# Two blocks on one core: what the order of TensorE's work does after a product on part of the array

## The chip, the cores and the metric

One core of a Trainium2 chip runs the whole program. The metric is the device time of one execution in microseconds; of the kernel before there are three runs.

## The reference, cut to what matters

256 tokens of width 1024 pass through two blocks, all in fp32. Only the parts that meet on TensorE are shown.

```
block 1:  h = rmsnorm(x);  proj = h @ w_in            # q k v z, dq dk dv
          gated delta rule, chunks of 64, 4 heads:    # "delta"
             A = I + strict(k_beta k^T * decay);  solve A [u|w] = rhs
             scan over 4 chunks: v_new = u - w S;  o = q S + a v_new;  S = S g + k^T v_new
          differential attention, 4 heads             # "diff heads"
          x += [o_la, o_d] @ w_out
          x += (silu(h @ w_gate) * (h @ w_up)) @ w_down
block 2:  mixer: gated linear attention in chunks ("gla"), block attention ("moba"), gates
          memory attention over 256 memory rows
          mixture of experts: 32 experts, 2 per token, each 1024 -> 512 -> 1024
```

## The kernel before, in words

**Dense products.** Every weight of the dense layers is fp32 and is split on chip into two fp32r parts, high and low (`Stream.split`: ScalarE rounds the high part, VectorE subtracts it for the low one). A product of activations and weights is then three matmuls: high x high, high x low, low x high. `job_ws`, `job_as`, `job_out`, `job_ffn` and `job_half` issue them in pieces of three, and give the turn back after each piece with `yield 0`. In the trace such a piece is three rows whose operands are `wh` or `wl` (weights) and `xTh`, `xTl`, `memTh` and the like; a piece has 256 or 512 columns per matmul. These jobs stand in one list, `self.jobs`, in the order of the weights' loads.

**Chains.** Everything between the dense layers (delta, diff heads, gla, moba, norms, softmax) is written as generators, called chains, which give the turn back where they have to wait. Many of their products use only part of the 128x128 array: `delta` works on chunks of 64 rows, so it multiplies 64x64 blocks on the rows 0 to 63 and 64 to 127, and the states of its scan are 64x128 or 128x64. Here such a product is called a part product, any other a dense one. In fp32 one product is two MATMUL rows, so eight products are a group of x16.

**Delta's inverse.** The triangular system is inverted by six levels of doubling (`for l in range(6)` in `delta`, L1208). In each level, for both row tiles t = 0 and 1, a first set of eight part products (`mks` by M, rows `im,mk`) goes to a bank, VectorE scales it to `pt` (rows `ipt`), and then a second set (rows `im,ipt` and `ipt,im`) and a VectorE subtraction give the next M (rows `im`). After the levels come `wT` and `u` (rows `im,kb` and `av,im`), and the scan over four chunks (rows `u,kd`/`vn,kd`, `u,KE`/`vn,KE`, `S,wT`, `S,qs`). `gla` has part products of the same sort (rows `gqs,gki`, `vg,gkdn`, `gS,gqe`).

**Who sets the order.** The program's order is fixed when it is built. `Pace` is a model of the engines: `note` (L201) charges each instruction a cost, remembers when each tensor is written (`wr`) and when each engine is free (`free`); `at` adds a latency, 205 ns from a VectorE write to TensorE. `drive` (L474) picks the next step: of the chains, in their order in the list, the first whose `ready` is not later than `now`, which is TensorE's planned free time plus 50 ns; if there is none, the first job goes on by one piece, unless a chain would be ready as early. A bare `yield` in a chain sets `ready` to the end of its step plus 200 ns (`advance`, L446), a `yield tensor` to the time at which the tensor is there for TensorE, `yield 0` to at once. So after a bare `yield` behind a product, a dense piece always goes in between, if there is one. The order on each engine's own queue is the order in which the steps are issued; `Stream.pump` puts the splits of the weights between them. The expert weights of the last part come through 22 buffers of 1 MB (`Experts`); its order is written out by hand, `drive` has no part in it.

Each row of the profile names line 249, since every instruction passes through one helper; so rows are told apart by their tiles.

Of the kernel before, what the change touches and what calls it, by code (L numbers as in the profile page):

```python
# [19 lines left out]
F32R = mybir.dt.float32r  # L20
# [14 lines left out]
class Pack:  # L35
    def __init__(self):
        self.off, self.n = {}, 0
        self.parts = []
# [93 lines left out]
TABLE = {AF.Exp: 0, AF.Ln: 1, AF.Silu: 2, AF.Sigmoid: 3}  # L132
TICK = 3413.0
NS1 = 178
NWARM = 18
NKEEP = 1
NAFT = 1
# [11 lines left out]
class Pace:  # L149
# [7 lines left out]
    def __init__(self):  # L157
        self.free = dict.fromkeys(("tensor", "vector", "scalar", "gpsimd", "sync"), 0.0)
        self.dma, self.step = 0.0, 0.0
        self.tick, self.full, self.cols = 0, False, 0.0  # L160
        self.table = None
        self.wr, self.rd = {}, {}

    def cost(self, eng, op, out, ins):
# [36 lines left out]
    def note(self, eng, op, args, kw):  # L201
        isap = lambda v: hasattr(v, "tensor") and hasattr(v, "ap")
        out = args[0]
        ins = [a for a in (*args[1:], *kw.values()) if isap(a)]
        t = self.free[eng]
        if op == "activation" and args[2] in TABLE and TABLE[args[2]] != self.table:
            t += 1283
            self.table = TABLE[args[2]]
        if op == "dma_start" and eng == "sync":
            t = max(t, self.dma)  # L210
        outs = [out] + [o for o in (kw.get("accum_out"),) if o is not None]
        if op == "tensor_tensor_reduce":
            outs.append(ins.pop())
        for a in ins:
            t = max(t, self.at(a, eng))
            if a.space == PSUM:
                t = max([t] + [e + 130 for o, e in self.rd.get(a.tensor.name, {}).items() if o != eng])
        for o in outs:
            t = max([t] + [e + (100 if n != eng else 0) for n, e in self.rd.get(o.tensor.name, {}).items()])
        if op == "dma_start":  # L220
            n = out.nbytes() / 360.0
            if eng == "sync":
                self.dma = self.free[eng] = t + n
            else:
                self.free[eng] = t + 1000
            end = t + n + 2000
        else:
            c = 165 * out.shape[-1] + 300 if kw.get("op") == ALU.pow else self.cost(eng, op, out, ins)
            if eng == "tensor":
                n, rows = out.free_size(), ins[0].shape[0]  # L230
                c = self.clock(t, c, n if rows < 128 else min(2.4 * c, 4 * n))
            end = self.free[eng] = t + c
        for o in outs:
            self.wr[o.tensor.name] = (end, eng)
        for a in ins:
            self.rd.setdefault(a.tensor.name, {})[eng] = end
        if op != "dma_start":
            self.step = max(self.step, end)
# [31 lines left out]
class Stream:  # L270
# [59 lines left out]
    def next(self, name):  # L330
        i = self.used
        assert self.pieces[i][0] == name, (self.pieces[i][0], name)
        while self.nsplit <= i:
            self.split()
        self.used += 1
        _, _, _, kk, n, _ = self.pieces[i]
        hi, lo = (w.rearrange("p (k n) -> p k n", n=n) for w in self.hl[i % HLB])
        return hi, lo, kk
# [87 lines left out]
class K:  # L426
# [47 lines left out]
    def drive(self, chains, until=None):  # L474

        until = until or chains
        chains = list(chains)
        while not all(c.done for c in until):
            chains = [c for c in chains if not c.done]
            self.jobs = [c for c in self.jobs if not c.done]  # L480
            self.S.pump()
            now = self.m.free["tensor"] + 50
            live = [c for c in chains if self.runnable(c)]
            best = next((c for c in live if c.ready <= now), None)
            if best is None:
                live += [c for c in self.jobs[:1] if self.runnable(c)]
                assert live, "no chain can go on"
                best = min(reversed(live), key=lambda c: max(c.ready, now))
            self.advance(best)
# [139 lines left out]
    def small(self, name):  # L629
        o, n = self.soff[name]  # L630
        return self.sml[0][:, o:o + n] if o < NS1 else self.sml[1][:, o - NS1:o - NS1 + n]

# [179 lines left out]
    def begin(self):  # L812
# [7 lines left out]
                    self.c2.tile([128, I["consts"].shape[1] - NC1], F32, name="cst2")]  # L820
        self.sml = [self.c2.tile([128, NS1], F32, name="sml1"),
                    self.c2.tile([128, I["small"].shape[1] - NS1], F32, name="sml2")]
        nc.sync.dma_start(self.cst[0], I["consts"][:, :NC1])
        for t, q in enumerate((nc.sync, nc.scalar)):
            q.dma_start(x[t], I["x"][0, t * 128:(t + 1) * 128, :])
        nc.sync.dma_start(self.sml[0], I["small"][:, :NS1])
        self.junk = self.c2.tile([128, 512], F32, name="junk")
        self.cut = self.c2.tile([128, 232], F32, name="cut")
        self.S = Stream(self, self.plan())
        self.S.load(2)  # L830
        nc.sync.dma_start(self.sml[1], I["small"][:, NS1:])
        nc.sync.dma_start(self.cst[1], I["consts"][:, NC1:])
        self.S.load()
        self.ident = self.const("ident")
        for _ in range(NWARM):
            self.mm(self.banks[0][:, :128], self.ones, self.ones, True, True)
# [1463 lines left out]
```

## Time and profile before

| what | value |
|---|---|
| runs of the kernel before | 1089.24, 1089.37, 1089.77 us (median 1089.37) |
| the profiled execution's own time | 1089.57 us |
| its span, first to last instruction | 1087.8 us |
| busy share: PE, PEld, DVE, ACT, POOL | 97%, 69%, 46%, 35%, 5% |
| mean granted TensorE clock | 0.997 of full speed |
| moved from and to HBM | 300 MB, mean 276 GB/s |
| chain that ended last | PE 61%, DMA 33%, DVE 2%, ACT 2% |

PE is the matmul side of TensorE, PEld its weight loads, DVE VectorE, ACT ScalarE, POOL GpSimd. A matmul's duration in the rows is longer than its distance to the next one, since matmuls are pipelined; what a matmul takes of TensorE's time is read from start to start. A row "x16" is a group of 16 matmuls; its start is the first one's.

### The profile page before, as it was taken

The numbers are of one execution on the slowest core, as the hardware profiler recorded it, in microseconds if no ns is written. First come the engines' busy times: TensorE is split into PE (matmuls) and PEld (weight loads), VectorE is DVE, ScalarE is ACT, GpSimd is POOL, SyncE is SP. The second block draws the span as 40 slices with busy tenths as digits, with TensorE's granted clock in tenths as the row PEclk, the third lists the DMA queues.
The fourth block names the chain that finished last, engine by engine and source line by source line (L and its number), as shares of the span: only waits on it lengthen the run. The fifth ranks groups of instructions, "written<-read, shape, count | busy, mean of one in ns | idle before, by whom it ended". The sixth has DMA issues, their size and how long they took to land.

```text
span 1087.8 us, 16591 instructions
## 1 busy us (share of the span) xinstructions
PE 1056.4 (97%) x6848; PEld 750.9 (69%) x6848; DVE 505.7 (46%) x919; ACT 383.5 (35%) x680; POOL 57.4 (5%) x86
## 2 busy tenths in 40 slices
PE   9999999999999999999999999999999998989995
PEld 8989788999999978889998754434443434334541
DVE  5777747665655568575577552222121212111121
ACT  6553536644434466566446430110000000000112
POOL 0145011000000010100000000000000000000000
PEclk9999999999999999999999999999999999999998
DMA  8453225576465535463559779999999999999994
GB/s 306 124 193 111 67 78 161 207 271 208 159 215 176 173 116 166 157 202 130 188 183 355 288 296 421 421 420 421 421 421 421 421 421 421 420 420 421 421 421 191
DMA packets 91100, 300.03 MB, mean 276 GB/s; under 512 B 4951, under 2 KB 33932, under 8 KB 67724
## 3 DMA queue, kind: packets, MB, share of 16 engines
q1 hardware_dynamic: 89564, 294.70, 71.1%
q0 software_dynamic: 1024, 3.17, 1.0%
q8 instruction: 56, 0.92, 0.3%
q10 hardware_dynamic: 432, 1.05, 0.3%
q14 instruction: 24, 0.20, 0.0%
HBM read 297.83 MB, written 1.07 MB: 275 GB/s over the span
## 4 chain that ended last, share of the span: by engine, by line
PE 61%; DMA 33%; DVE 2%; ACT 2%; issue 1%; POOL 0%; SPq 0%; ACTq 0%; DVEq 0%
PE bank L249 61%; DMA wm<-in_w_exp_up 20%; DMA wm<-in_w_exp_down 13%; ACT junk L249 1%; DMA x<-in_x 0%; DVE cy L249 0%; DVE junk L249 0%; DVE xTl L249 0%; ACT wh L249 0%; DVE x L249 0%; ACT xTh L249 0%; ACT sg L249 0%; ACT wm L249 0%; DVE dp L249 0%; POOL nr L249 0%
## 5 line engine op out<-in xcount | busy, mean ns | idle before, releaser
L249 DVE TENSOR_TENSOR wl<-wr,wh 128x1024 fp32r<-128x1024 f32 (+1 forms) x175 | 211.2, 1223 | 134.2 <-ACT wh L249 130.9
L249 PE MATMUL bank<-wm,xe 128*64 128x512 f32 x1024 | 231.7, 596 | 3.3 <-DMA wm<-in_w_exp_up 3.3
L249 PE MATMUL bank<-xTh,wh 128*128 128x256 f32 x768 | 223.1, 291 | 0.0
L249 ACT ACTIVATE wh<-wr 128x1024 fp32r<-128x1024 f32 (+1 forms) x175 | 180.1, 1050 | 118.4 <-PE bank L249 102.8
L249 PE MATMUL bank<-xTl,wh 128*128 128x256 f32 x768 | 217.3, 283 | 0.8 <-DVE xTl L249 0.8
L249 PE MATMUL bank<-xTh,wl 128*128 128x256 f32 x768 | 217.2, 283 | 0.2 <-DVE wl L249 0.2
L249 PEld LDWEIGHTS bank<-wm,xe 128*64 128x64 f32 x1024 | 74.7, 137 | 137.4 <-issue 123.4
L249 PEld LDWEIGHTS bank<-xTh,wh 128*128 128x128 f32 x768 | 147.0, 191 | 4.6 <-issue 2.4
L249 PEld LDWEIGHTS bank<-xTl,wh 128*128 128x128 f32 x768 | 147.1, 192 | 2.3 <-DVE xTl L249 1.2
L249 PEld LDWEIGHTS bank<-xTh,wl 128*128 128x128 f32 x768 | 147.0, 191 | 0.4 <-DVE wl L249 0.4
L249 PE MATMUL bank<-wm,hdT 128*64 128x512 f32 x512 | 118.7, 594 | 8.9 <-DMA wm<-in_w_exp_down 7.6
L249 DVE TENSOR_TENSOR sg<-bank,sg 128x512 f32<-128x512 f32 x16 | 11.1, 692 | 187.5 <-PE bank L249 187.5
L249 PEld LDWEIGHTS bank<-wm,hdT 128*64 128x64 f32 x512 | 39.7, 137 | 82.7 <-issue 64.4
L249 ACT ACTIVATE sg<-bank 128x512 f32<-128x512 f32 x20 | 11.9, 597 | 198.3 <-PE bank L249 198.2
L249 DVE SCALAR_TENSOR_TENSOR ys<-bank,ws,ys 128x512 fp32r<-128x512 f32 x32 | 24.0, 751 | 114.7 <-ACT ys L249 113.0
L249 ACT ACTIVATE ys<-bank,ws 128x512 fp32r<-128x512 f32 x32 | 22.0, 687 | 152.0 <-PE bank L249 152.0
L249 POOL TENSOR_TENSOR nr<-nr,mhalf 128x2 f32<-128x2 f32 (+1 forms) x9 | 6.0, 673 | 670.8 <-DVE nr L249 670.7
L249 PEld LDWEIGHTS bank<-ys,pwT 128*128 128x128 f32 x128 | 22.7, 188 | 18.5 <-issue 11.4
L249 PE MATMUL bank<-wl,fhh 128*128 128x512 f32 x88 | 35.2, 400 | 0.0
L249 PE MATMUL bank<-ys,pwT 128*128 128x512 f32 x128 | 34.6, 410 | 0.5 <-DVE ys L249 0.5
L249 PE MATMUL bank<-wh,fhh 128*128 128x512 f32 x88 | 34.8, 395 | 0.0
L249 PE MATMUL bank<-wh,fhl 128*128 128x512 f32 x88 | 34.5, 392 | 0.0
(384 smaller groups left out, 1445.4 us busy)
## 6 DMA issues: line engine op xcount, KB each, us to landing
wm<-in_w_exp_gate SPq DMA_DIRECT2D x64, 1024.0 KB, 19.8
wm<-in_w_exp_up SPq DMA_DIRECT2D x64, 1024.0 KB, 19.8
wm<-in_w_exp_down SPq DMA_DIRECT2D x62, 1024.0 KB, 19.8
wr<-in_w_in SPq DMA_DIRECT2D x33, 1024.0 KB, 5.2
wr<-in_w_gate_up SPq DMA_DIRECT2D x22, 1024.0 KB, 5.3
wr<-in_w_down SPq DMA_DIRECT2D x11, 1024.0 KB, 5.2
wr<-in_w_out SPq DMA_DIRECT2D x8, 1024.0 KB, 5.1
wr<-in_w_ckv SPq DMA_DIRECT2D x4, 1024.0 KB, 7.4
```

The source lines that it names most:

```text
L249: r = f(*args, **kw)
```

## The change: how chains and pieces are ordered, and what a change of kind costs in the plan

`note` now classes each TensorE instruction: dense, if it contracts over more than 64 rows and is a transpose, has more than 64 columns of weights, or is fp32r; otherwise it is a product on part of the array. An instruction whose class differs from the one before is charged 115 ns more. And `drive` moves `now` 150 ns later for the chains, if TensorE's last planned instruction was a part product.

```
+NEAR = 150
...
-        self.table = None
+        self.table, self.dense, self.was = None, True, True
...
             if eng == "tensor":
                 n, rows = out.free_size(), ins[0].shape[0]
-                c = self.clock(t, c, n if rows < 128 else min(2.4 * c, 4 * n))
+                self.dense = rows > 64 and (op == "transpose" or ins[0].shape[-1] > 64 or ins[0].dtype == F32R)
+                c = self.clock(t, c, n if rows < 128 else min(2.4 * c, 4 * n)) + (115 if self.dense != self.was else 0)
+                self.was = self.dense
             end = self.free[eng] = t + c
...
             live = [c for c in chains if self.runnable(c)]
+            if not self.m.dense:
+                now += NEAR
             best = next((c for c in live if c.ready <= now), None)
```

No instruction's shape, data or count is changed by it; only the order in which the steps are issued can be.

## Rows read from the trace of the kernel before

**Rows 1.** Windows: us; busy us (count) of each engine; clock, DMA share, GB/s.
```profile
0.00:640.00 640.00, 631.81 (x4812) 568.51 (x4813) 412.00 (x726) 335.11 (x602) 56.26 (x84) 1.00 0.56 188
640.00:645.00 5.00, 5.00 (x29) 2.02 (x29) 4.25 (x5) 2.61 (x3) 0.00 (x0) 1.00 0.00 0
645.00:1062.00 417.00, 405.78 (x1956) 175.20 (x1952) 84.21 (x180) 39.68 (x63) 0.00 (x0) 1.00 1.01 420
```

**Rows 2.** Waits of PE up to 640 us: us in total, times, longest.
```profile
PE bank L249 <- DVE x L249: 1.6, 1, 1.6
...
PE bank L249 <- POOL nr L249: 0.2, 1, 0.2
```

**Rows 3.** Windows of delta's inverse, its scan, the mixer, and one unbroken part stretch.
```profile
68.00:118.00 50.00, 50.00 (x736) 44.65 (x735) 34.55 (x59) 20.44 (x39) 22.43 (x30) 1.00 0.43 138
118.00:165.00 47.00, 46.75 (x337) 36.69 (x336) 29.84 (x90) 24.55 (x73) 5.19 (x6) 1.00 0.20 68
400.00:510.00 110.00, 109.95 (x786) 96.78 (x787) 75.38 (x152) 70.48 (x133) 9.30 (x18) 1.00 0.50 161
157.20:162.90 5.70, 5.70 (x43) 4.12 (x41) 2.71 (x11) 0.98 (x5) 0.00 (x0) 1.00 0.00 0
```

**Rows 4.** Timeline of PE, delta's inverse: start us, us, engine, line, operation, tiles.
```profile
69.33 0.50 PE L249 MATMUL bank<-wh,xTh 128*128 128x512 f32 x1
...
103.05 0.68 PE L249 MATMUL bank<-im,ipt 64*64 64x64 f32 x16
103.56 0.63 PE L249 MATMUL bank<-ipt,im 64*64 64x64 f32 x16
104.13 0.39 PE L249 MATMUL bank<-xTh,wh 128*128 128x256 f32 x1
104.35 0.28 PE L249 MATMUL bank<-xTl,wh 128*128 128x256 f32 x1
104.47 0.28 PE L249 MATMUL bank<-xTh,wl 128*128 128x256 f32 x1
104.68 0.68 PE L249 MATMUL bank<-im,ipt 64*64 64x64 f32 x16
...
106.30 0.68 PE L249 MATMUL bank<-im,mk 64*64 64x64 f32 x16
106.92 0.39 PE L249 MATMUL bank<-xTh,wh 128*128 128x256 f32 x1
...
115.89 0.39 PE L249 MATMUL bank<-xTh,wh 128*128 128x256 f32 x1
```

**Rows 5.** Timeline of DVE in the same stretch.
```profile
102.61 1.23 DVE L249 TENSOR_TENSOR wl<-wr,wh 128x1024 fp32r<-128x1024 f32 x1 [1.45 <-PE bank L249]
...
105.87 0.69 DVE L249 TENSOR_TENSOR im<-im,bank 128x512 f32<-128x512 f32 x1 [0.94 <-PE bank L249]
107.03 0.42 DVE L249 TENSOR_TENSOR ipt<-bank,lastat 128x256 f32<-128x256 f32 x1 [0.47 <-PE bank L249]
```

**Rows 6.** Timeline of PE, delta's second half.
```profile
128.74 0.50 PE L249 MATMUL bank<-wh,xTh 128*128 128x512 f32 x1
...
136.96 1.08 PE L249 MATMUL bank<-u,KE 64*64 64x128 f32 x8
137.97 1.09 PE L249 MATMUL bank<-S,wT 128*64 128x128 f32 x8
...
143.37 1.08 PE L249 MATMUL bank<-vn,KE 64*64 64x128 f32 x8
144.38 0.50 PE L249 MATMUL bank<-wh,xTh 128*128 128x512 f32 x1
...
154.01 0.39 PE L249 MATMUL bank<-memTh,wh 128*128 128x256 f32 x1
```

**Rows 7.** Timeline of PE, the mixer's gla.
```profile
436.68 0.65 PE L249 MATMUL bank<-vg,gkdn 64*64 64x128 f32 x8
437.27 0.50 PE L249 MATMUL bank<-wh,xTh 128*128 128x512 f32 x1
```

## The prediction, made before the changed kernel was built or run

> **What bounds the kernel now.** I read the windows first, cut where the expert part begins. Up to 640 us TensorE is busy for 631.8 of 640 us while the DMA engines are at 0.56; from 645 to 1062 us the DMA engines are full at 420 GB/s and stay so [rows 1]. Between them lie 5 us with no DMA at all [rows 1]: all 22 expert buffers are full and wait for the first one to be used up. So the second half is a fixed amount of loading that cannot begin before TensorE has come to the experts, and every microsecond that TensorE saves or loses before 640 us moves the end by the same amount. Next the waits of PE up to 640 us: twelve, from 1.6 down to 0.2 us, each seen once or twice [rows 2]. TensorE does not wait for others there; what it can save is time in which it is busy and does no useful work. The stages with part products are three, and PE is busy in them for 50.0 of 50, 46.75 of 47 and 109.95 of 110 us [rows 3]. So the timeline of PE, start to start, is the view that decides.
>
> **What an interposed piece costs.** In the inverse the second set of tile 0 (103.05 and 103.56) is followed by a dense piece, and that by the second set of tile 1 at 104.68 [rows 4]. The first group of 16 takes 0.51 us when another part group follows it. From 103.56 to 104.68 are 1.12 us; one group of 0.51 and three dense matmuls at the 0.12 us that stand between 104.35 and 104.47 make 0.87. So 0.25 us are lost: 0.06 on the way out of the part group, 0.10 at the first dense matmul (0.22 instead of 0.12) and 0.09 on the way back (0.21 instead of 0.12). Behind a first set the way out costs more: 106.30 to 106.92 is 0.62 against 0.51, so 0.11 [rows 4], and the loss 0.30. I take 0.28 for each piece that no longer stands between two part products. The three dense matmuls themselves are not saved: the piece is done later, in a row of others.
>
> **Where the change removes one.** A bare `yield` behind a part product made the chain ripe 200 ns after TensorE's free time, while `drive` looked 50 ns ahead; now it looks 200 ns ahead, so the chain goes on at once. Whether that brings two part products together depends on what the next step needs. I went through the chains in their order:
>
> - Inverse, between the tiles: the second set of tile 1 needs only `pt` of tile 1, finished long before. Six levels, six pieces. In level 0 the first set of tile 1 needs nothing, and in levels 1 and 2 M of tile 1 is old, as long runs of dense work stand before them: three more pieces. From level to level (three places with a single piece) tile 0's first set needs M of tile 0. That makes 12 pieces, the first at 69.33, the last at 115.89 [rows 4].
> - The last three have a wait. A set begun at 106.30 is through at 106.81 (0.51 later), and VectorE begins with it at 107.03, so 0.22 later [rows 4, 5]. Its subtraction takes 0.69 us [rows 5], the plan allows 0.205 us on to TensorE: 1.12 us, of which tile 1's two groups cover 2 x 0.51. About 0.1 us is waited. Sum for the inverse: 12 x 0.28 - 3 x 0.1 = 3.1 us.
> - From the first sets to tile 0's second set the evacuation takes 0.22 + 0.42 us [rows 5] plus 0.2, of which the other first set covers 0.51. If the plan bridges it, TensorE stands for about 0.33 us in place of losing 0.30: nothing, either way. The first set of tile 1 in levels 3 to 5 needs a fresh M and keeps its piece.
> - Delta's second half: eight pieces (three of them transposes of a diff head) go, the first at 128.74, the last at 154.01 [rows 6]: between `wT` and `u`, `u` and `wT`, `u` and the scan, `kd` and `KE`, `wT` and `qs`. After the first `KE` the scan needs a fresh S, so the piece removed in front of that `KE` comes back behind it: not counted.
> - Here the two classes of the planner are too few. `KE` (64x64) followed by `S,wT` (128x64) takes 1.01 us, and followed by a dense matmul also 1.01 us [rows 6]. Going from one part form to another costs what going to a dense one costs. Of the eight places six join unlike forms, so one change of about 0.10 stays: 6 x 0.18 + 2 x 0.28 = 1.6 us.
> - gla: three pieces between like forms, one between the two `gqs,gki` sets and two between the `vg,gkdn` sets, as at 437.27 [rows 7]: 3 x 0.28 = 0.8 us. `qkm`, `pT,vm` and `gS,gqe` stay, since the next step waits for a softmax, or there is none.
>
> The Trainium skill speaks to the fifth point ("TensorEngine Tiling (Array Packing)", section Key Properties): changing the tiling mode drains TensorE, and it means any mode, not only a step from part to whole. The trace agrees with its 1.01 against 1.01 us. If the planner's two classes were right instead, the sum would be 0.6 us larger.
>
> **What it adds.** The later `now` holds for every chain behind a part product, also for one whose next step is dense: TensorE then stands up to 150 ns longer without a part product to gain. About 30 of the 57 part stretches that the timeline has up to 640 us keep a piece behind them; I put 0.5 us on this, between 0 and 30 x 0.15 = 4.5. The instructions queued behind such a wait are only dense pieces, for which nobody waits. The 115 ns are no work; they make the plan's TensorE slower, by 57 x 0.23 = 13 us over the stage if all stayed, near the 0.25 to 0.30 measured. This moves many decisions between chains and splits; I put nothing on it, with 2 us to either side, which is what a handful of shifted pieces and waits as in [rows 2] amount to.
>
> Sum: 3.1 + 1.6 + 0.8 - 0.5 = 5.0 us, all on the path, as TensorE never waits and the DMA stream follows it. The profiled execution took 1089.57 us (1.8 outside its span), 0.2 above the median of the runs; so 1084.6 by its own time, 1084.4 against the median. A difference under 0.2% (2.2 us) I count as none.
>
> **Rivals.**
>
> 1. *The pieces come back.* A chain that goes on sooner meets its next real wait sooner, and a piece is put there; only what needs nothing is gained (the six between the tiles and three in gla, 2.5 us, less the 0.5 for waits and up to 2 of shifted order). Time 1087 to 1089.4, say 1088.3. For it: S and M are fresh after every second set. Against it: pieces already stand at those real waits, and a longer run there costs one loss, not two.
> 2. *Late operands, slower.* The plan charges 80 ns for a product that takes 0.51/8 = 64 ns [rows 4]. It believes a set of eight to last 0.13 us longer than it does, and so bridges waits longer than 200 ns; and VectorE works in order, with splits of 1.23 us [rows 5] in front of the evacuations. Each piece taken out is 0.36 us of cover gone. It decides where the wait at the some 23 places exceeds 0.28 us on average. If one in three stands behind a split: 8 x 1.23 = 9.8, less 5.5 gained, so 4.3 us slower: 1093.7. Against it: the plan counts VectorE's queue, and PE hardly waits today [rows 2].
> 3. *The clock falls.* Longer stretches of small part products with waits between them could lower the granted clock from 2.4 to 1.2 GHz. If half of the inverse's 50 us ran so, 25 us of work would take 50: 25 us less 5, 1109. Against it: 1.00 in all three stages, and in 5.7 us of part products without one dense piece [rows 3].
> 4. *More than counted.* A plan with dearer changes also sets fewer pieces at the waits I call even; five more at 0.28 and no waits: 1081.8.
>
> **How the numbers follow.** Forecast 0.55, rival 1 0.22, rival 2 0.13, rival 3 0.03, rival 4 0.07. The forecast's own range is 1082.0 to 1087.2. With rival 1 and the near end of rival 2 the range is 1081.5 to 1090.0. Faster: the forecast, rival 4 and a little of rival 1, 0.64; the same: most of rival 1, 0.21; slower: 0.15.
>
> **What would show it.** In the changed trace: MATMUL counts unchanged; in the inverse the second sets of both tiles back to back (two groups `im,ipt`/`ipt,im` with no `wh` row between); fewer part stretches, about 34 to 40 in place of 57; the first `wm` matmul about 5 us before its 640; the DMA stream at 420 GB/s for as long as before, with all of the gain ahead of it. Rival 2 shows as new PE waits for DVE `ipt` or `im`, rival 3 as a clock under 1.00 between 68 and 165. I am wrong if the stretches are fewer but the experts start no earlier.

## The result: slower, and where the time went

The changed kernel takes 1098.99 us (six runs, 1096.32 to 1101.99), the kernel before 1089.55. The ratio is 1.0088, with an interval of 1.0078 to 1.0098: 0.9% slower, where 0.5% faster was forecast. The six runs stand in two groups, 1096.3 to 1096.9 and 1101.1 to 1102.0 us, with mean granted clocks of 0.995 and 0.987, so the median lies between them, where no run is; the profile is of the first (1096.68 us, span 1094.9).

First the windows of the changed kernel, cut where its experts begin, as [rows 1] and [rows 3].

```profile
0.00:647.50 647.50, 627.11 (x4816) 568.33 (x4816) 413.66 (x726) 336.50 (x603) 51.90 (x84) 0.99 0.55 186
647.50:652.00 4.50, 4.50 (x23) 1.63 (x24) 4.39 (x5) 2.10 (x2) 0.00 (x0) 1.00 0.00 0
652.00:1069.00 417.00, 405.55 (x1956) 175.33 (x1950) 84.13 (x180) 39.68 (x63) 0.00 (x0) 1.00 1.01 420
68.00:118.00 50.00, 46.41 (x735) 43.03 (x731) 38.77 (x69) 22.03 (x44) 17.82 (x28) 1.00 0.40 128
118.00:165.00 47.00, 40.15 (x298) 33.79 (x297) 24.72 (x70) 21.13 (x62) 6.98 (x8) 0.96 0.19 58
131.00:138.00 7.00, 1.73 (x19) 1.29 (x18) 3.89 (x18) 3.72 (x14) 2.03 (x2) 0.96 0.06 23
137.40:140.80 3.40, 2.85 (x14) 2.86 (x15) 1.17 (x3) 0.00 (x0) 0.00 (x0) 0.51 0.00 0
400.20:403.70 3.50, 3.50 (x19) 3.50 (x18) 2.60 (x7) 1.87 (x6) 0.00 (x0) 0.51 0.00 0
```

The second half is as it was: 417 us of loading at 420 GB/s behind some 5 us without DMA. The experts begin 6.9 us later (647.50 against 640.64), and the span is 7.1 us longer; so the loss lies ahead of them, as the gain was expected to. TensorE, which was busy in all but 0.25 us of delta's second half [rows 3], is now idle there for 6.9 of 47 us. Next the waits of PE up to 660 us, five of seventeen (twelve before, none over 1.6 us [rows 2]).

```profile
PE bank L252 <- DVE lay L252: 5.3, 1, 5.3
PE bank L252 <- DVE x L252: 3.3, 1, 3.3
PE bank L252 <- DVE dp L252: 1.4, 2, 0.9
PE bank L252 <- ACT vT L252: 1.4, 2, 1.2
...
PE bank L252 <- DVE ipt L252: 0.9, 3, 0.4
```

The pieces did go. This is the timeline of PE in the inverse, answering to [rows 4]: four groups of the second sets without a dense row between them, and tile 1's first set (104.64) straight into tile 0's second set.

```profile
101.45 0.68 PE L252 MATMUL bank<-im,ipt 64*64 64x64 f32 x16
101.97 0.63 PE L252 MATMUL bank<-ipt,im 64*64 64x64 f32 x16
102.43 0.63 PE L252 MATMUL bank<-im,ipt 64*64 64x64 f32 x16
102.90 0.63 PE L252 MATMUL bank<-ipt,im 64*64 64x64 f32 x16
103.48 0.68 PE L252 MATMUL bank<-im,mk 64*64 64x64 f32 x16
...
104.64 0.68 PE L252 MATMUL bank<-im,mk 64*64 64x64 f32 x16
105.16 0.63 PE L252 MATMUL bank<-im,ipt 64*64 64x64 f32 x16
```

Up to the experts 25 part stretches are left of 57, and not the 34 to 40 expected: too many went. From 120.39 to 146.24 us no dense piece stands at all. Here is the timeline of that stretch, PE first, then what the other engines did while PE waited.

```profile
120.39 1.11 PE L252 MATMUL bank<-im,kb 64*128 64x64 f32 x16
121.42 1.09 PE L252 MATMUL bank<-av,im 64*64 64x128 f32 x16
...
126.60 1.09 PE L252 MATMUL bank<-S,wT 128*64 128x128 f32 x8
127.53 1.04 PE L252 MATMUL bank<-S,qs 128*64 128x128 f32 x8
...
131.01 1.66 PE L252 MATMUL bank<-dqk 64*128 64x128 f32 x16
137.95 1.97 PE L252 MATMUL bank<-S,wT 128*64 128x128 f32 x8 [5.27 <-DVE lay L252]
...
146.24 0.50 PE L252 MATMUL bank<-wh,xTh 128*128 128x512 f32 x1
```

```profile
132.40 1.28 ACT L252 ACT_TABLE_LOAD   x1
133.69 0.17 ACT L252 ACTIVATE le<-bank 128x2 f32<-128x2 f32 x1
133.89 0.16 DVE L252 TENSOR_TENSOR nlam<-le 128x1 f32<-128x1 f32 x1 [3.25 <-ACT le L252]
...
134.67 1.02 POOL L252 TENSOR_TENSOR hf<-hf,mhalf 128x4 f32<-128x4 f32 x1 [5.63 <-DVE hf L252]
...
136.76 1.13 DVE L252 SCALAR_TENSOR_TENSOR lay<-bank,hf,zs 128x128 f32<-128x128 f32 x4
```

The scan's norm runs through ScalarE, VectorE, GpSimd and VectorE again before `lay` has read the bank that the next `S,wT` writes (by the code, delta gives that bank back behind `lay`, and takes it again). The table load and the first head's constants stand ahead of it in the same queues. In the kernel before, dense pieces ran meanwhile, from 144.38 on [rows 6]. Here nothing was put there. The granted clock is at 1.00 through 12 us of part products and falls to half only at 137.4, when TensorE has stood for 4.8 us, for 3.4 us; again at 400.3, behind the 3.3 us wait for `x`.

Why did the planner put no piece there, though it prefers one to waiting? The plan's own times say it. In the plan of the changed kernel, as it is built, the eight score products `dqk` of head 0 end at 137.82 planned us, and `S,wT` begins at 138.12. On the chip `dqk` was through at 132.7 (131.01 + 1.66), and `S,wT` began at 137.95. For the plan the hole was 0.3 us and not 5.3: its `clock` charged TensorE double.

```
plan's TensorE at half speed, in planned us up to the experts (from 3.5 us on)
before:   587.1 to 590.5
changed:  102.3 to 112.6, 122.8 to 150.2, 375.6 to 378.9, 607.1 to 610.6
the eight dqk products of head 0:  132.66 to 137.82 planned us, 1.66 us on the chip
```

`clock` halves the plan's speed behind a stretch of planned time in which it has counted too few columns. A product on 64 rows counts 0.3 to 1.0 columns in a planned ns (64 in 214 ns for `im,kb`, 128 in 128 for `av,im`), a dense matmul 2.4 (519 in 216); the 115 ns count none and take planned time. With the pieces gone and the 115 ns added the count fell short, from there on everything looked ready to a TensorE believed slow, and so still fewer pieces were set: the plan's error feeds itself. If the plan goes on at full speed all the same (e1 below), the count falls short for 6.9 planned us twice (from 102.3 and from 119.3), where the changed kernel's plan has 10.3 and 27.5.

### The profile page after: what moved, and what is told of

Same layout as the page of the kernel before. It is cut to its first block, busy times and chain, and to the rows that moved or that the text cites. A ratio compares the mean times of both kernels' runs of the same rounds, so it can differ in the third digit from the quotient of the medians.

```text
span 1094.9 us, 16583 instructions
## 1 busy us (share of the span) xinstructions
PE 1051.0 (96%) x6848; PEld 750.5 (69%) x6848; DVE 507.4 (46%) x919; ACT 384.4 (35%) x680; POOL 53.0 (5%) x86
## 4 chain that ended last, share of the span: by engine, by line
PE 66%; DMA 24%; DVE 5%; ACT 3%; issue 1%; SPq 0%; POOL 0%; ACTq 0%; DVEq 0%
PE bank L252 66%; DMA wm<-in_w_exp_up 14%; DMA wm<-in_w_exp_down 9%; DVE wl L252 1%; ACT wh L252 1%; ACT junk L252 1%; DVE cy L252 1%; DMA x<-in_x 0%; DVE junk L252 0%; DVE xTl L252 0%; DVE x L252 0%; ACT L252 0%; ACT smp L252 0%; DVE memTl L252 0%; DVE gla L252 0%
## 5 line engine op out<-in xcount | busy, mean ns | idle before, releaser
L252 ACT ACTIVATE wh<-wr 128x1024 fp32r<-128x1024 f32 (+1 forms) x175 | 179.6, 1048 | 102.3 <-PE bank L252 84.1
```

Source lines behind the costliest of these rows:

```text
L252: r = f(*args, **kw)
```

## Experiments

The theories: **A**, the plan's clock (above). **B**, waiting in place of a dense piece is a loss by itself. **C**, the chip's clock falls because of the longer part stretches. What the variants gave, with the start of the first `cst,nr` matmul behind block 1's attention and of the first expert matmul, in us (the kernel before ran beside every set of variants, with medians of 1089.42 to 1089.55; part stretches up to the experts):

| kernel | part stretches | attention ends | experts begin | time |
|---|---|---|---|---|
| before | 57 | 201.43 | 640.64 | 1089.4 |
| changed | 25 | 206.55 | 647.50 | 1099.0 |
| e1 changed, plan's clock full | 33 | 197.49 | 635.40 | 1084.5 |
| e2 NEAR alone | 34 | 199.05 | 638.87 | 1088.5 |
| e3 115 ns alone | 54 | 213.23 | 654.30 | 1103.3 |
| e4 NEAR alone, plan's clock full | 36 | 195.48 | 633.35 | 1082.1 |
| e5 plan's clock full alone | 57 | 201.29 | 640.48 | 1089.5 |
| e6 115 ns alone, plan's clock full | 58 | 203.60 | 642.84 | 1091.7 |
| e7 as e4, NEAR = 149 | 56 | 202.09 | 641.15 | 1090.3 |
| e8 before, plan forced to half | 57 | 204.94 | 647.91 | 1097.4 |
| e9 changed, plan's clock full early | 33 | 197.64 | 638.82 | 1087.6 |
| e11 as e4, NEAR = 300 | 36 | 205.64 | 643.50 | 1093.1 |

**e1 to e4: the two halves of the change, with and without the plan's clock.** In e1 and e4 `clock` never halves after the plan's first 7 us:

```
-        return c if self.full else 2 * c
+        return c if self.full or k > 1 else 2 * c
```

e2 and e4 leave out ` + (115 if self.dense != self.was else 0)`; e3 sets `NEAR = 0`.

e1: 

> The changed kernel, whose planner now never charges TensorE at half speed after its first stretch (clock() returns the full cost). In the changed kernel's own plan TensorE runs at half speed from 102 to 113 and from 123 to 150 planned us, while the chip's granted clock is 1.00 until 137 us. Theory A (the plan believes in a slow TensorE, so it takes late operands for ready and sets no dense piece in front of them; this made the 5.3 us wait of PE for DVE lay): that wait is under 1 us, dense pieces stand between 131 and 146 us, and the time is 1083 to 1088 us, faster than the kernel before. Theory B (waits in place of dense pieces are a loss by themselves, whatever the plan's clock): the waits for DVE ipt, im, dp and lay stay, 1093 us or more. Theory C (the chip's own clock falls because of long part stretches): two or more stretches at 0.5 again and 1094 us or more.

e2: 

> The later now (NEAR = 150) without the 115 ns for a change of kind. Its plan is at half speed only from 119 to 140 planned us, so some 20 us instead of 38. Theory A: part of the loss, 1090 to 1097 us, with a PE wait of 2 to 5 us in the scan of delta. Theory B: as the whole change, 1096 to 1100, because NEAR is what sets the waits. If the 115 ns alone were at fault: 1084 to 1086.

e3: 

> The 115 ns for a change of kind without the later now (NEAR = 0). The 115 ns take planned time and add no columns to the plan's count, so its plan falls to half speed from 96 to 130 and 136 to 160 planned us, longest of all, though the dense pieces stay between the part products. Theory A: slower than before, 1091 to 1098, with new PE waits where the plan is at half speed. Theory B: no NEAR, no waits: 1088 to 1090, the same as before, or a little faster since the plan's times are nearer to the chip's.

e4: 

> NEAR = 150 without the 115 ns, and the plan's TensorE never at half speed after its first stretch. Theory A: the gain that was forecast, 1083 to 1087 us; with e2 it shows what the plan's clock alone costs. Theory B: 1093 or more. Theory C: stretches at 0.5 in the scan, and 1094 or more.

Measured: e1 1084.54 us, ratio to before 0.9956 (0.9944 to 0.9969); e4 1082.14, 0.9934 (0.9921 to 0.9947); e2 1088.45, 0.9999 (0.9988 to 1.0010), its runs spread from 1087.25 to 1092.91; e3 1103.26, 1.0130 (1.0115 to 1.0145). The order of the four is A's and not B's, but only e1 and e4 lie in A's ranges: e2 came out better than its 1090 to 1097 (the longest wait of PE in delta's second half is 1.7 us, where 2 to 5 were expected), and e3 worse than its 1091 to 1098. That e3 is the slowest of all is the sharpest of these: it has no NEAR, its dense pieces stand where they stood before (54 stretches), and 115 ns that exist only in the plan cost 14 us. In e1 the hole is full: behind `KE` the timeline of PE has 21 dense matmuls, 5.0 us of them, before the next `S,wT`.

```profile
131.12 1.08 PE L252 MATMUL bank<-vn,KE 64*64 64x128 f32 x8
132.14 0.50 PE L252 MATMUL bank<-wh,xTh 128*128 128x512 f32 x1
132.47 0.39 PE L252 MATMUL bank<-wl,xTh 128*128 128x512 f32 x1
...
136.81 0.39 PE L252 MATMUL bank<-wh,xTl 128*128 128x512 f32 x1
137.12 0.43 PE L252 MATMUL bank<-S,wT 128*64 128x128 f32 x2
```

e4 has the same second sets back to back as the changed kernel, and between 60 and 165 us one wait of PE in all:

```profile
102.59 0.68 PE L252 MATMUL bank<-im,ipt 64*64 64x64 f32 x16
103.10 0.63 PE L252 MATMUL bank<-ipt,im 64*64 64x64 f32 x16
103.57 0.63 PE L252 MATMUL bank<-im,ipt 64*64 64x64 f32 x16
104.04 0.63 PE L252 MATMUL bank<-ipt,im 64*64 64x64 f32 x16
```

```profile
PE bank L252 <- ACT wT L252: 0.2, 1, 0.2
```

C is a consequence, not the start. In e3 the chip's clock does fall, for 10.2 and for 3.4 us in delta's second half, but ahead of the first fall TensorE stood: the windows show 1.97 us busy in the 3.6 us before it. Ahead of the second, too, stand two waits for `dp`, of 0.5 and 0.4 us.

```profile
123.00:126.60 3.60, 1.97 (x10) 1.21 (x10) 2.64 (x5) 2.51 (x4) 0.00 (x0) 1.00 0.00 0
...
126.60:136.80 10.20, 10.18 (x55) 8.03 (x55) 5.72 (x27) 4.86 (x14) 0.00 (x0) 0.50 0.31 103
```

As a part of the loss the fallen clock is not small, though. In the changed kernel, `S,wT` takes 0.93 us at the upper level (126.60 to 127.53) and 1.76 at the lower (137.95 to 139.71), so work at half speed lasts about twice as long. By this, an estimate, the 13.6 us at half speed cost e3 some 6.8 of the 11.8 us by which its attention ends later than before. In the changed kernel the waits weigh more: up to the end of the attention its waits of PE behind 40 us sum to 10.9 us, against 2.2 in e1, and its 3.4 us at half speed cost 1.7 at most, of 9.1 us between the two.

**e5 and e6: controls.** e5 is the kernel before with the line of `clock` above, e6 is e3 with it.

e5: 

> The kernel before with nothing changed but the plan's clock, which is never at half speed after its first stretch. The plan of the kernel before is at half speed once, from 587 to 591 planned us, so almost no step can move. Theory A: 1088.5 to 1090 us, no difference; then what e1 and e4 gained is not owed to the plan's clock by itself. If it gains 2 us or more by itself, e1 and e4 have to be read again.

e6: 

> The 115 ns without the later now, and the plan's TensorE never at half speed after its first stretch; beside e3 (1103 us) only the plan's clock differs. Theory A: the harm of the 115 ns goes through the plan's clock alone, so 1087 to 1090 us, no PE wait over 1 us in delta. Theory B (the dearer change misplaces pieces by itself): 1094 to 1103.

Measured: e5 1089.50, ratio 1.0001 (0.9992 to 1.0010): the line of `clock` is worth nothing by itself. e6 1091.71, 1.0021 (1.0012 to 1.0030). So of the 14 us in e3, 11.6 go through the plan's clock (1103.26 less 1091.71), but 2.3 do not; A had said none, and e6 lies outside A's range and outside B's. About as much, 2.4 us, stands between e1 and e4. In e6 two waits account for 1.5 of it, `ipt` 1.1 and `dp` 0.4 us, which e5 does not have; that with a dearer TensorE in the plan operands seem ready earlier than they are is argued from the code and was not tested.

**e7: where the gain of e4 sits.** `NEAR = 149` in e4.

> As e4 (1082 us), but NEAR is 149 and not 150. A bare yield makes a chain ripe 200 ns after TensorE's planned free time; 50 + 149 falls one ns short of it, so dense pieces stand again between the part products (53 part stretches up to the experts, as before). If the gain is in the pieces behind bare yields, as forecast: 1088 to 1090 us, no gain. If it is in bridging waits of any length up to 200 ns: 1083 to 1086.

Measured: 1090.30, 1.0008 (0.9999 to 1.0017), with 56 part stretches (57 before, by the same count). One ns of the plan's look-ahead takes away all of e4's gain: it lies in the pieces behind bare yields, as the prediction had it. Bridging the other waits, of up to 199 ns, gains nothing: e7 is 0.9 us slower than before.

**e8: the converse.** The kernel before, with the plan's clock forced to half in one stretch:

```
-        return c if self.full else 2 * c
+        return c if self.full and not 123e3 < t < 150e3 else 2 * c
```

> The kernel before, without NEAR and 115 ns; only its plan's TensorE is charged at half speed from 123 to 150 planned us, as the changed kernel's plan is. All it can do is to move steps. Theory A: a plan that believes in a slow TensorE is enough, 1091 to 1097 us, with new PE waits for DVE or ACT between 125 and 165 us. Theory B (it takes NEAR): 1089 to 1090.

Measured: 1097.35, ratio 1.0084 (1.0070 to 1.0097), just above A's range. By the profiled runs it is the same loss as the change's, 7.2 us against 7.1 over the kernel before, without NEAR and without 115 ns. The attention part ends 3.5 us later, with two new waits of PE there,

```profile
PE bank L249 <- DVE dp L249: 1.7, 2, 1.4
PE bank L249 <- DVE dy L249: 1.2, 2, 1.0
```

and the rest comes behind it: all planned times are later, `clock` draws its line elsewhere and halves the plan from 368 to 372 planned us, and PE waits 3.7 us for `x` instead of 1.6, with the chip's clock at half for 3.4 us behind it (from 395.8).

**e9: the second place.** The plan's clock kept full up to 250 planned us alone.

```
+        return c if self.full or 1 < k and t < 250e3 else 2 * c
```

> The changed kernel with the plan's clock kept full only up to 250 planned us, so over the whole of block 1's attention; behind that the plan may halve it again, and does from 356 to 362 planned us, where the feed-forward part ends and the next norm begins. There the changed kernel has a PE wait for DVE x of 3.3 us (1.6 in the kernel before) and the chip's clock at 0.5 for 3.4 us behind it. Theory A (the same mistake in a second place): the attention part as in e1, the wait for x 3.3 to 3.7 us and the stretch at 0.5 back, so 1086.5 to 1089 us, 2 to 4 over e1. If the second place has another cause: as e1, 1084 to 1085.

Measured: 1087.57, 0.9979 (0.9970 to 0.9988), 3.0 over e1. The attention ends within 0.2 us of e1's. The wait for `x` is back at 3.3 us (1.6 in e1), and the chip's clock is at half for 3.4 us from 391.0. So the same error strikes at two places: by the profiles, 9.1 us of the change's loss against e1 lie in the attention (206.55 against 197.49) and 3.0 behind it. What makes the count fall short at the second place is not the 115 ns or missing pieces: ahead of the norm TensorE is idle for 2.6 us in the plans of the kernel before, the changed one, e1 and e9 alike, and only where `clock` draws its line, which moves with all planned times, decides whether a stretch with this hole counts too little.

**e10: the changed kernel again.**

> The changed kernel once more. Its six runs fell into two groups, 1096.3 to 1096.9 us at a mean granted clock of 0.995 and 1101.1 to 1102.0 at 0.987. If the difference is the chip's clock behind long PE waits, each 0.001 of mean clock is some 0.6 us at this span, the two groups come again with the same clocks, and a profile at the lower clock has more than two stretches at 0.5 up to the experts.

Measured: 1098.95, in the same two groups (1095.7 to 1095.9 at 0.994, 1102.0 to 1102.2 at 0.986 to 0.987). Its profile is again of the first group; here the half-speed stretch behind the wait for `lay` lasts 6.8 us (from 135.5), and the one at 400 is missing, though PE waits 3.3 us for `x` there as before. So the same program with the same waits does not always have the same falls of the clock. Where the second group has its further time at half speed was not seen: open, and so is the expectation of more than two stretches.

**e11: how far the bridging can go.** `NEAR = 300` in e4.

> As e4 (1082 us), with NEAR = 300: chains ripe up to 350 ns after TensorE's planned free time go on behind a part product. If what is gained lies in bare yields alone, longer waits only replace a loss of 0.28 us for each interposed piece by a wait of about as much: 1081.5 to 1083.5. If longer waits are a loss: 1083.5 to 1086.

Measured: 1093.08, 1.0034 (1.0022 to 1.0045): a miss on either count. PE waits for `av`, `u` and `wT` (1.3, 0.8 and 0.3 us), and behind these waits the chip's clock is at half for 13.7 us, the longest such stretch of all. So B is not wrong everywhere: with the plan's clock full, bridging longer waits loses too, 10.2 us up to the end of the attention (205.64 against 195.48 in e4), of which the slow clock is some 6.4 by the estimate above (half of 12.74 us busy).

```profile
123.50:127.00 3.50, 1.88 (x22) 1.60 (x24) 2.87 (x3) 1.48 (x3) 0.00 (x0) 1.00 0.32 68
127.00:140.70 13.70, 12.74 (x72) 10.34 (x69) 3.46 (x16) 6.51 (x21) 1.03 (x1) 0.50 0.16 60
```

Rival 3 of the prediction is real, then, and as it said, in stretches with waits between; without them it did not come: the changed kernel's 12 us of part products without a wait ran at 1.00.

## Why the prediction was wrong

- *The bound* was right: every variant's time follows the start of its experts (e4: 7.3 us earlier, time 7.3 lower; the changed kernel: 6.9 later, profiled time 7.1 higher).
- *The pieces between part products* were right in place and somewhat small in size. e4 has 21 stretches fewer than before, 23 were counted; its gain is 7.3 us, or 0.35 for each, where 0.28 was taken. Of it 6.0 us are in the attention (forecast 3.1 + 1.6 less 0.5) and 1.2 in gla (forecast 0.8). The waits charged against it hardly came: 0.2 us between 60 and 165 us.
- *Like and unlike forms*: `im,kb` followed by `av,im` takes 1.03 us in the changed kernel, and 1.04 followed by a dense matmul in the kernel before (127.70 to 128.74); `S,wT` followed by `S,qs`, of the same form, 0.93 against 1.02 (137.97 to 138.99). The rule drawn from [rows 6] holds.
- **The step that failed** is "The 115 ns are no work; [...] I put nothing on it, with 2 us to either side". The plan's clock, which stands in the listing above the prediction, was not weighed: the 115 ns and the missing pieces together lower the count of columns on which `clock` decides. Where it falls short the plan charges double, and TensorE stood where the plan saw it at work: 5.3 us for `lay`, 3.3 for `x`. That is worth 12.3 us by the profiled runs (1096.68 against 1084.38 in e1) and 14.4 by the medians, the changed kernel's lying between its two groups. A further 2.4 us are the 115 ns by themselves (e1 against e4). With the plan's clock kept full the whole change comes to 1084.54, and 1084.4 was forecast; that is luck, since two errors in it, 2.3 us too little for the pieces and 2.4 too little for the 115 ns, cancel.
- *Rival 2* had the sign and the kind, late operands behind a plan that is wrong about TensorE, but not the place: it looked for a small wait at each of 23 places, from a product charged 80 ns for 64. The loss is one wait of 5.3 us, one of 3.3 and smaller ones, from products charged as much as three times what they take (`dqk`: 5.16 us for 1.66).
- *Rivals 1 and 4*: the pieces did not come back; with the plan's clock full the gain forecast for them is there (e4). Rival 4's 1081.8 does not come out of its own terms: five pieces at 0.28 are 1.4 us and no waits 0.8, which makes 1082.2.

The rows of the kernel before on which the third point rests, beside those of [rows 6]:

```profile
127.70 1.11 PE L249 MATMUL bank<-im,kb 64*128 64x64 f32 x16
...
138.99 0.55 PE L249 MATMUL bank<-cst,dp 128*128 128x128 f32 x3
```

What stays open: the second group of runs (e10), and 0.8 of the 2.3 us of the 115 ns in e6.

## What to carry to other kernels

A planner that sets the order is part of the kernel: when a change touches its costs, ask first which of its own thresholds the new costs can cross, since a fictitious cost moves real work. A filler between two dependent steps is worth removing only where the next operand is ready; look for the longest stretch that loses its filler, and not for the average one. Test a planned order by its own times beside the trace: where the trace waits up to about the moment that the plan had set (137.95 against 138.12 us here), look for a wrong cost in the plan before you look for a slow engine.

## What the runs showed of the hardware that was not expected

The granted clock held its upper level (2.4 GHz) through 12 us of small part products without a dense one, and up to the experts it fell to the lower (1.2 GHz) only in or behind waits. In the changed kernel it fell when TensorE had stood for 4.8 us, in the second profile of the same program (e10) after 3.3 us; in e3 and e11 behind stretches in which TensorE was busy for 1.97 of 3.6 us and for 1.88 of 3.5. A wait did not always bring a fall: behind the same 3.3 us wait for `x` the changed kernel was at half for 3.4 us, and e10 not at all.

How long the lower level lasted varied just as much: 3.4 us in the changed kernel, with part products behind the first fall and dense work behind the second; 6.8 us in e10, with the same part products; 10.2 in e3 and 13.7 in e11. What sets the length is not shown. In e3 and e11 some 1.6 us of standing were cheaper than what came behind them, 5.1 and 6.4 us by the estimate above; in the changed kernel the wait of 5.3 us was the dearer.
